# First attention heads in one set of streams with the recurrent half's output tiles

## The chip, the cores and the metric

One core of a Trainium2 chip runs the whole program. The time is device microseconds of one execution; the number given for the kernel before is the median of three. Engines are named as the profile names them: PE (TensorE: matmuls and transposes), DVE (VectorE), ACT (ScalarE), POOL (GpSimd), SP (SyncE, which issues the DMAs). PE writes its results to PSUM, which has eight banks here, each holding 128 x 512 float32.

## What is computed

One layer of a hybrid streaming encoder over 1024 prompt frames and 8 x 16 sample frames, together 1152 rows, or nine tiles of 128 rows (eight of the prompt, the ninth holds all samples). Cut to what matters:

```python
xr, gate, q, k, v, qi, ki, wi = split(rmsnorm(x) @ w_in)      # 1024 -> 2376 columns
y_a = rglru(conv(xr)) * gelu(gate)                            # recurrent half, 512 wide
q, k = rope(rmsnorm(q)), rope(rmsnorm(k))                     # 8 query heads, 2 key heads of 64
sel = topk(sum_h relu(qi_h . ki) * wi_h, 256)                 # sparse: the keys each frame may see
y_b = softmax(q . k[sel] / 8) @ v[sel]                        # attention half, 512 wide
x = x + concat(y_a, y_b) @ w_out                              # 1024 x 1024
x = x + (silu(h @ w1) * (h @ w2)) @ w_ffn_out                 # h = rmsnorm(x)
```

The attention is causal in chunks of 64 frames, so a query tile i of the prompt needs the key tiles 0 to i and no other. For query tiles 0 and 1 there are at most 256 keys, so no selection is needed and a fixed mask serves; tiles 2 to 8 need the mask that the top-k search makes.

## The kernel before, in words

The program is unrolled. Python generators, called streams, emit the instructions; `run(streams, width, side)` (line 93) keeps `width` streams active, always steps the oldest one that is due by its own estimate of time, and between the steps gives a turn to the side streams (weight loader, top-k search, key rotation, query normalisation and others). A stream that ends makes room for the next in the list. What comes out is an order of priority; a planner with a cost model of its own then fixes the order of instructions on each engine, allocates buffers and places the waits. On the chip each engine follows that order.

Stages, by time in the profile: normalisation and keys, index scores, then the recurrent half with the query projections beside it (to 408 us), then the output tiles of the recurrent half (408 to 474 us), the attention heads (474 to about 660 us), the output tiles of the attention half, and the feed-forward part (719 us to the end).

The pieces that the change touches:

- `out_tile_a(i)` (line 1341): the rows i of `y_a` times the upper half of `w_out`. Eight float32 matmuls 128x128 by 128x512 into two PSUM banks (each shows as two records in the trace), then two DVE additions into `acc[i]`. The four weight tiles `wa` hold four of the eight 4 KB slots of the pool `wr` until tile 8 is done. The last addition of tile 8 is kept as `wa_last`: the masks of tiles 6, 7 and 8 are emitted only once it exists, and on DVE are ordered behind it.
- `k_rope` (line 1249): a side stream that for each key tile i applies the rotation on POOL and DVE, writes the keys out, transposes them on PE and splits them into high and low parts, by two ACT copies and two DVE subtractions for each of the two key heads, into `k1` and `k2`. At the end `k_done` is set.
- `q_norm` (line 1236): multiplies the nine query tiles by their inverse norms on POOL.
- `attn(i, kv)` (line 1388): four query heads of query tile i on one key head. It waits until `k_done`, its mask and its queries are there. Then for each of the four: score matmuls, a DVE pass that adds the mask, scales and takes the maximum (`m`, `mx`), an exponential on ACT, a reciprocal on DVE, a multiplication on POOL. Then for each key tile: four PE transposes of `m`, a split by ACT and DVE, and three matmuls with the values; one ACT copy to `yF` ends it. The rows `m` take two of the `wr` slots where the width is at most 512, four above, and are taken in turn (`m_turn`).
- `sample_attn(b)`: the same for the 16 frames of stream b, against its cache.

The stage before the change runs as two calls: nine output tiles two at a time with `k_rope` and `q_norm` as side streams, a loop that drains these two, and then 24 heads and samples four at a time (`ATT_ORDER`: the heads of query tiles 0 to 5 first, those of 6 and 7 between the samples).

The key buffers `k1` and `k2` are allocated after the pool `tq` of the query projections is closed. Pools are stacked, so the keys stand where `tq`'s tiles stood (`tab`, `rp` and others of `q_tile`), and the first write to them waits for the last rotation of a query tile.

Of the kernel before, what the change touches and what calls it, by code (L numbers as in the profile page):

```python
# [10 lines left out]
F32R = mybir.dt.float32r  # L11
# [10 lines left out]
NT = 9  # L22
NP = 8
# [7 lines left out]
NB = 8  # L31
# [50 lines left out]
class Kernel:  # L82
# [183 lines left out]
    def build(self, upto=99):  # L266
        ctx, tc, nc, I, O = self.ctx, self.tc, self.nc, self.I, self.O
        L = "left"
        R = "right"
# [29 lines left out]
        def close():  # L299
            for st in (kist, tka, mid, yst, right):  # L300
                st.close()

        side = [self.loader()]
        with tc.tile_pool(name="t1a", bufs=2, side=R) as tp:
            g, wk = self.load_kv_weights(tp)
            side = self.run([self.norm_kv(i, tp, g, wk) for i in range(NT)], self.W_NORM, side)
# [7 lines left out]
        self.scored, self.masked, self.tk_done = set(), {0, 1}, set()  # L314
        self.qst, self.qst_t = {}, {}
        self.n_lru, self.spare, self.wa_last = 0, None, None
        self.m_turn, self.m_next, self.n_sa, self.in_att, self.k_done = 0, 0, 0, False, False
        self.n_idx, self.n_sidx, self.sidx, self.sq_done = 0, 0, None, False
        topks = [self.topk(g, p) for g, p in zip(groups, self.TK_PACE)]
        side += topks  # L320
# [1 line left out]
        with tc.tile_pool(name="t1b", bufs=2, side=R) as tp:  # L322
            self.qs = tp.tile([64, NB, 8, TS], F32, name="qs", bufs=1)
            st = {**{i: self.index(i, tp) for i in range(2, NT)}, **{("s", b): self.sample_index(b) for b in range(NB)}}
            side = self.run([st[x] for x in self.INDEX_ORDER], self.W_IDX, side + [self.sample_sel()])
# [6 lines left out]
        with tc.tile_pool(name="tq", bufs=2, side=R) as tp:  # L332
            queries = [[self.clock, g] for g in self.q_proj(tp)]
            with tc.tile_pool(name="lru", bufs=1, side=R) as lp:
                self.phase = 1
                side = self.run(self.lru(lp), 3, [self.lru_prep(lp)] + side, queries)
            self.phase = 2
            prep, lo = self.out_room(), self.lru_out()
            side = [x for x in self.run([g for _, g in queries], 3, [prep, lo] + side) if x is not prep]
# [4 lines left out]
        self.k1 = k_p.tile([128, 2, 1024], F32R, name="k1")  # L344
        self.k2 = k_p.tile([128, 2, 1024], F32R, name="k2")
        self.ksT = k_p.tile([128, 2, 128], F32R, name="ksT")
        with tc.tile_pool(name="woa", bufs=2, side=R) as tp:
            self.phase = 3
            kr, qr = self.k_rope(tp), self.q_norm(tp)
            side = self.run([self.out_tile_a(i) for i in range(NT)], 2, [prep] + side + [kr, qr])  # L350
            for x in (kr, qr):
                for _ in x:
                    pass
                side = [y for y in side if y is not x]
        if upto < 4:
            return close()
        with tc.tile_pool(name="att", bufs=1, side=R) as tp:
            self.in_att = True
            self.phase = 4
            self.smp = self.hblk.tile([128, 3 * D], F32, tag="h", name="smp")  # L360
            self.pT_free = [self.rest[:, 2048:3072]] + [self.smr[:, k * 1024:(k + 1) * 1024] for k in range(3)]
            self.pTn = tp.tile([128, 2, 128], F32R, name="pTn")
            self.kn1 = self.kn.rearrange("p i d -> p (i d)")
            self.mask01 = self.kn1[:, 896:1152]
            nc.gpsimd.memset(self.mask01, 0.0)
            nc.gpsimd.memset(self.mask01[0:64, 192:256], -BIG)
            st = {**{("s", b): self.sample_attn(b, tp) for b in range(NB)},
                  **{(i, kv): self.attn(i, kv, tp) for i in range(NP) for kv in range(2)}}
            self.smp_in = None
            side = self.run([st[x] for x in self.ATT_ORDER], self.W_ATT, side + [self.sample_prep()])  # L370
        mid.close()
        tka.close()
        if upto < 5:
# [3 lines left out]
        with tc.tile_pool(name="wob", bufs=2, side=R) as tp:  # L377
            self.gf = tp.tile([128, D], F32, name="gffn", bufs=1)
            nc.sync.dma_start(self.gf, I["norm_ffn"][None, :].to_broadcast([128, D]))
            self.half_b, self.hf_done, self.w1_first, self.first_ps = 0, set(), [], {}  # L380
            self.run([self.out_tile(i, tp) for i in range(NT)] + [self.ffn_start()], self.W_OUT,
                     [self.out_prep()] + side + [self.ffn_first()])
# [29 lines left out]
    LRU_LAT = 3.0  # L412
    K_LAT = 5.0
    W_ATT = 4
    W_OUT = 4
    INDEX_ORDER = (8, 2, 3, 4, ("s", 0), ("s", 1), 5, ("s", 2), ("s", 3), 6, ("s", 4), ("s", 5), 7, ("s", 6), ("s", 7))
    ATT_ORDER = (tuple((i, k) for i in range(6) for k in range(2)) + tuple(x for b in range(4) for x in ((6 + b // 2, b % 2), ("s", 2 * b), ("s", 2 * b + 1))))
# [831 lines left out]
    def k_rope(self, tp):  # L1249
        nc, I, O = self.nc, self.I, self.O  # L1250
        gk = self.load_g(tp, I["k_norm"], "gk")
        yield self.K_LAT
        v = self.kss.rearrange("p i a -> p (i a)")
        self.newton_rsqrt(v, v, tp, 2 * NT)
        rs = self.kss
        yield 0.5
        for i in range(NT):
            tab = self.tables(tp, i, gk, 1)
            self.begin()
            o = self.kn[:, i, :].rearrange("p (h d) -> p h d", h=2)  # L1260
            self.rope(o, o, tab, 2, tp, bufs=1)
            self.pool_tt(o, o, rs[:, i, :, None].to_broadcast([128, 2, 64]), ALU.mult)
            of = o.rearrange("p h d -> p (h d)")
            dst = O["k_p"][0, i * 128:(i + 1) * 128] if i < NP else O["k_s"].rearrange("b t k d -> (b t) k d")
            nc.sync.dma_start(dst.rearrange("t k d -> t (k d)"), of)
            t = self.end()
            yield 0.0
            yield from self.until(t)
            pt = self.ps()
            self.tr(pt[:, 0:128], of)  # L1270
            sl = slice(i * 128, (i + 1) * 128)
            if i == NP:
                self.split(self.ksT, pt[:, 0:128])
                self.k_done = True
                return
            for kv in range(2):

                a = slice(64 * kv, 64 * kv + 64)
                b = slice(64 - 64 * kv, 128 - 64 * kv)
                same, other = (self.k1, self.k2) if kv == 0 else (self.k2, self.k1)  # L1280
                h = same[a, kv, sl]
                nc.scalar.activation(h, pt[a, 0:128], AF.Copy)
                nc.scalar.activation(other[b, kv, sl], pt[a, 0:128], AF.Copy)
                nc.vector.tensor_tensor(other[a, kv, sl], pt[a, 0:128], h.bitcast(F32), op=ALU.subtract)
                nc.vector.tensor_tensor(same[b, kv, sl], pt[a, 0:128], h.bitcast(F32), op=ALU.subtract)
            yield 2.0


# [52 lines left out]
    def out_tile_a(self, i):  # L1341

        nc = self.nc
        nc.sync.dma_start(self.acc[i], self.x_src(i))
        w = []
        pos = [self.ps(), self.ps()]
        for c in range(4):
            w += yield from self.wait_w(("wa", c))
            for q in range(2):
                self.mm4(pos[q], self.yF[:, c, i * 128:(i + 1) * 128], w[c][:, q * 512:(q + 1) * 512], c == 0, c == 3)  # L1350
            yield 0.0
        if i == NT - 1:
            self.wused -= 4
        for q in range(2):
            a = self.acc[i][:, q * 512:(q + 1) * 512]
            x = nc.vector.tensor_tensor(a, pos[q], a, op=ALU.add)
            if q and i == NT - 1:
                self.wa_last = x.ins
            yield 0.4 if q else 0.0

    def out_tile(self, i, tp):
# [26 lines left out]
    def attn(self, i, kv, tp):  # L1388
# [2 lines left out]
        nch = 1 if W <= 512 else 2  # L1391
        n = W // nch
        mask = self.mask01[:, 256 - W:] if i < 2 else self.s[i]
        while not self.k_done or i not in self.masked or i not in self.q_ok or (kv and i not in self.qst):
            yield 0.5
        if kv == 0:
            self.begin()
# [355 lines left out]
```

## Time and profile before

| | |
|---|---|
| Median of three runs | 1537.71 us (1537.52 to 1539.65) |
| Profiled execution, its own time | 1536.94 us |
| Profiled execution, its span | 1535.1 us |
| PE busy | 1467.9 us (96%), 7786 matmuls |
| DVE busy | 865.2 us (56%) |
| ACT busy | 619.2 us (40%) |
| POOL busy | 269.7 us (18%) |
| Mean granted PE clock | 0.98 |

The chain that ended last goes through PE for 72% of the span and through DVE for 13%. A busy PE is not PE at its peak: the ends of matmuls are modelled, and a matmul at half clock counts as busy for twice the time, so the busy share has to be read beside the granted clock. The time of the profiled execution is 1.84 us more than its span.

### The profile page before, as it was taken

What the parts mean: (1) busy time and instruction counts of PE and PEld (TensorE: products, weight loads), DVE (VectorE), ACT (ScalarE), POOL (GpSimd) and SP (SyncE); (2) the same over time, 40 slices, a digit from 0 to 9 for tenths busy, and PEclk for the clock granted to TensorE, in tenths of its full rate; (3) what the DMA queues carried; (4) which work ended last, traced back from release to release, by engine and by line L of the source; (5) the groups of instructions that cost most, each with busy time, mean ns of one, the idle gap of its engine ahead of it and who ended that gap; (6) DMA issues with size and microseconds to landing.
All of it is one profiled execution on the core that took longest, in us unless ns stands there. A gap on an engine that the chain in (4) does not pass through costs nothing.

```text
span 1535.1 us, 20876 instructions
## 1 busy us (share of the span) xinstructions
PE 1467.9 (96%) x7786; PEld 1307.5 (85%) x7786; DVE 865.2 (56%) x1904; ACT 619.2 (40%) x1481; POOL 269.7 (18%) x425
## 2 busy tenths in 40 slices
PE   6889899889997999999999999999999999999998
PEld 6877688778745788889999998989898989898987
DVE  7556899899967988777233333342424242515233
ACT  5447988977415877745202020202121212111100
POOL 4214234333774544300000000000000000000000
PEclk8999899999998999999999999999999999999999
DMA  7201110010401002122102020202021111111003
GB/s 241 58 18 30 48 38 22 12 31 32 176 28 28 1 15 69 28 69 82 56 0 83 0 83 1 83 5 79 18 66 28 56 42 42 50 34 56 28 1 123
DMA packets 95093, 75.24 MB, mean 49 GB/s; under 512 B 13380, under 2 KB 85828, under 8 KB 94992
## 3 DMA queue, kind: packets, MB, share of 16 engines
q1 hardware_dynamic: 94992, 73.91, 15.9%
q8 instruction: 61, 1.00, 0.3%
q14 instruction: 40, 0.33, 0.1%
HBM read 67.62 MB, written 6.27 MB: 48 GB/s over the span
## 4 chain that ended last, share of the span: by engine, by line
PE 72%; DVE 13%; ACT 6%; issue 5%; POOL 2%; DMA 1%; SPq 0%; ACTq 0%; DVEq 0%; POOLq 0%
PE ps L207 66%; DVE junk L66 4%; PE ps L217 3%; ACT jk L66 3%; PE ps L212 3%; DVE tk_cand L66 2%; DVE tr L66 1%; ACT L66 1%; POOL rp L66 1%; DVE ti L66 1%; DVE qn L66 1%; ACT tr L66 1%; DVE m L66 1%; ACT relu L66 1%; DVE s L66 1%
## 5 line engine op out<-in xcount | busy, mean ns | idle before, releaser
L207 PE MATMUL ps<-hf,w 128*128 128x384 f32 x2556 | 453.1, 334 | 0.0
L207 PEld LDWEIGHTS ps<-hf,w 128*128 128x128 f32 x2556 | 444.2, 188 | 0.7
L207 PE MATMUL ps<-w,a 128*128 128x512 f32 x999 | 238.4, 389 | 0.0
L66 DVE TENSOR_TENSOR acc<-ps,acc 128x512 f32<-128x512 f32 x234 | 161.0, 690 | 118.2 <-PE ps L207 117.4
L207 PEld LDWEIGHTS ps<-w,a 128*128 128x128 f32 x999 | 187.3, 188 | 38.5
L66 ACT ACTIVATE w<-raw 128x512 fp32r<-128x512 f32 x124 | 75.2, 628 | 295.7 <-PE ps L207 219.2
L66 DVE TENSOR_TENSOR sg<-ps,sg 128x384 f32<-128x384 f32 x66 | 36.8, 557 | 276.7 <-PE ps L207 276.1
L66 ACT ACTIVATE a<-sg 128x384 fp32r<-128x384 f32 x66 | 34.5, 523 | 219.4 <-DVE sg L66 219.4
L66 DVE TENSOR_TENSOR w<-raw,w 128x512 fp32r<-128x512 f32 x116 | 76.9, 688 | 81.7 <-ACT w L66 81.5
L207 PE MATMUL ps<-hf,rest 128*128 128x384 f32 x612 | 114.3, 334 | 0.0
L66 ACT ACTIVATE jk<-s,tk_cand 128x384 bf16<-128x384 f32 (+3 forms) x128 | 99.5, 777 | 32.4 <-DVE tk_cand L66 29.7
L207 PEld LDWEIGHTS ps<-hf,rest 128*128 128x128 f32 x612 | 106.9, 188 | 0.2
L207 PE MATMUL ps<-h,w 128*128 128x384 f32 x576 | 106.7, 342 | 0.0
L207 PEld LDWEIGHTS ps<-h,w 128*128 128x128 f32 x576 | 100.4, 188 | 3.9 <-ACT relu L66 0.2
L207 PE MATMUL ps<-w,h 128*128 128x256 f32 (+1 forms) x600 | 97.7, 320 | 0.0
L207 PEld LDWEIGHTS ps<-w,h 128*128 128x128 f32 x600 | 85.1, 194 | 6.5
L66 ACT ACTIVATE sg<-ps 128x384 f32<-128x384 f32 x66 | 32.0, 486 | 119.7 <-PE ps L207 119.7
L212 PE MATMUL ps<-wa,yF 128*128 128x512 f32 x144 | 63.4, 593 | 2.4 <-DVE k L66 1.5
L66 POOL TENSOR_SCALAR m<-m,mx 128x128 f32<-128x128 f32 (+7 forms) x64 | 51.7, 814 | 54.1 <-DVE mx L66 45.2
L212 PEld LDWEIGHTS ps<-wa,yF 128*128 128x128 f32 x144 | 26.5, 190 | 35.5 <-issue 31.9
L66 ACT ACTIVATE m<-m,mx 128x128 f32<-128x128 f32 (+7 forms) x64 | 49.3, 771 | 16.4 <-DVE mx L66 16.0
L207 PE MATMUL ps<-k,qeo 128*128 128x384 f32 (+5 forms) x192 | 51.9, 383 | 3.7 <-DVE qeo L66 2.9
(266 smaller groups left out, 2139.8 us busy)
## 6 DMA issues: line engine op xcount, KB each, us to landing
raw<-in_w_ffn_in_dram SPq DMA_DIRECT2D x44, 512.0 KB
raw<-in_w_ffn_out_dram SPq DMA_DIRECT2D x22, 512.0 KB
raw<-in_w_in_dram SPq DMA_DIRECT2D x16, 512.0 KB
out_dram<-acc SPq DMA_DIRECT2D x9, 512.0 KB
x<-in_x_prompt_dram SPq DMA_DIRECT2D x8, 512.0 KB
acc<-in_x_prompt_dram SPq DMA_DIRECT2D x8, 512.0 KB
tab<-in_rope_dram SPq DMA_DIRECT2D x43, 64.0 KB
wa<-in_w_out_dram SPq DMA_DIRECT2D x4, 512.0 KB
```

The costliest lines, as they stand in the source:

```text
L66: return f(*args, **kw)
L207: self.nc.tensor.matmul(out, lhsT, rhs, start=start, stop=stop)
L212: self.nc.tensor.matmul(out, lhsT, rhs, start=start, stop=stop)
L217: self.nc.tensor.transpose(out, in_, self.ident[0:n, 0:n])
```

## The change

The two calls of `run` become one. The list begins with three output tiles (`OUT_FIRST`), then heads and output tiles alternate for six pairs, and the other heads and samples follow; four streams are active throughout. `k_rope` and `q_norm` stay side streams and are not drained. A head no longer waits for `k_done` but only until `k_tiles`, counted up as each key tile is split, is above its own query tile's number. The pool `att` is opened beside `woa`. The fixed mask `mask01` moves from the last columns of `kn` (key tiles 7 and 8, now still in use) to the end of `smp`. The phase number changes to 4 with the last output tile.

```diff
-        self.m_turn, self.m_next, self.n_sa, self.in_att, self.k_done = 0, 0, 0, False, False
+        self.m_turn, self.m_next, self.n_sa, self.k_done, self.k_tiles = 0, 0, 0, False, 0
...
-        with tc.tile_pool(name="woa", bufs=2, side=R) as tp:
+        with tc.tile_pool(name="woa", bufs=2, side=R) as tp, tc.tile_pool(name="att", bufs=1, side=R) as ap:
             self.phase = 3
-            kr, qr = self.k_rope(tp), self.q_norm(tp)
-            side = self.run([self.out_tile_a(i) for i in range(NT)], 2, [prep] + side + [kr, qr])
-            for x in (kr, qr):
-                for _ in x:
-                    pass
-                side = [y for y in side if y is not x]
-        if upto < 4:
-            return close()
-        with tc.tile_pool(name="att", bufs=1, side=R) as tp:
-            self.in_att = True
-            self.phase = 4
...
-            self.pTn = tp.tile([128, 2, 128], F32R, name="pTn")
+            self.pTn = ap.tile([128, 2, 128], F32R, name="pTn")
...
-            self.mask01 = self.kn1[:, 896:1152]
+            self.mask01 = self.smp[:, 2816:3072]
...
-            side = self.run([st[x] for x in self.ATT_ORDER], self.W_ATT, side + [self.sample_prep()])
+            outs, heads = [self.out_tile_a(i) for i in range(NT)], [st[x] for x in self.ATT_ORDER]
+            n = NT - self.OUT_FIRST
+            order = outs[:self.OUT_FIRST] + [x for p in zip(heads[:n], outs[self.OUT_FIRST:]) for x in p] + heads[n:]
+            side = self.run(order, self.W_ATT, [prep] + side + [self.k_rope(tp), self.q_norm(tp), self.sample_prep()])
...
+    OUT_FIRST = 3
...  # k_rope, behind the splits of a key tile
+            self.k_tiles += 1
...  # out_tile_a, with the last output tile
+                self.phase = 4
...  # attn
-        while not self.k_done or i not in self.masked or i not in self.q_ok or (kv and i not in self.qst):
+        while self.k_tiles <= i or i not in self.masked or i not in self.q_ok or (kv and i not in self.qst):
```

## Rows read from the trace of the kernel before

**Rows 1.** The page, part 2: busy tenths in 40 slices of 38.4 us; PEclk is the granted clock.

```profile
PE   6889899889997999999999999999999999999998
DVE  7556899899967988777233333342424242515233
PEclk8999899999998999999999999999999999999999
```

**Rows 2.** Busy time by stage, instructions in brackets; then granted PE clock, DMA share, GB/s.

```profile
408.00:443.00 35.00, 34.08 (x84) 15.00 (x83) 28.42 (x50) 2.59 (x14) 33.68 (x50) 1.00 0.09 25
443.00:474.00 31.00, 29.52 (x75) 13.06 (x74) 18.38 (x53) 7.73 (x30) 6.37 (x19) 1.00 0.16 45
474.00:520.00 46.00, 34.65 (x172) 28.07 (x171) 42.06 (x131) 35.76 (x94) 28.11 (x39) 0.81 0.02 6
520.00:640.00 120.00, 115.38 (x748) 100.70 (x747) 99.01 (x284) 92.69 (x216) 54.39 (x64) 1.00 0.12 36
```

**Rows 3.** The chain that ended last, in order of time: start, length, what.

```profile
719.30 811.35 PE ps L207 x4311
```

**Rows 4.** PE in order of time, 408 to 449 us; idle time and releaser in square brackets.

```profile
408.00 13.90 PE L212 MATMUL ps<-wa,yF 128*128 128x512 f32 x32
421.74 0.27 PE L217 MATMUL ps<-ident,kn 128*128 128x128 f32 x1
...
426.58 7.03 PE L212 MATMUL ps<-wa,yF 128*128 128x512 f32 x16
433.45 0.27 PE L217 MATMUL ps<-ident,kn 128*128 128x128 f32 x1
433.56 7.03 PE L212 MATMUL ps<-wa,yF 128*128 128x512 f32 x16
440.43 0.27 PE L217 MATMUL ps<-ident,kn 128*128 128x128 f32 x1
...
445.61 3.67 PE L212 MATMUL ps<-wa,yF 128*128 128x512 f32 x8 [1.48 <-DVE k L66]
```

**Rows 5.** PE in order of time, the first heads, 477 to 491 us.

```profile
477.69 4.57 PE L207 MATMUL ps<-k,qeo 128*128 128x128 f32 x18 [2.95 <-DVE qeo L66]
...
484.85 0.48 PE L217 MATMUL ps<-ident,m 128*128 128x128 f32 x1 [2.59 <-POOL m L66]
...
490.09 0.33 PE L217 MATMUL ps<-ident,m 128*128 128x128 f32 x1 [2.17 <-POOL m L66]
```

**Rows 6.** ACT in order of time, 421 to 447 us: the only row there.

```profile
441.92 4.02 ACT L66 ACTIVATE k<-ps 64x128 fp32r<-64x128 f32 x14 [32.13 <-DVE qn L66]
```

**Rows 7.** DVE in order of time, 437 to 447 us.

```profile
437.85 0.68 DVE L66 TENSOR_TENSOR acc<-ps,acc 128x512 f32<-128x512 f32 x1
...
441.33 0.43 DVE L66 TENSOR_TENSOR qn<-qn,rp 128x256 f32<-128x256 f32 x1
442.50 0.58 DVE L66 TENSOR_TENSOR k<-ps,k 64x128 fp32r<-64x128 f32 x2 [0.74 <-ACT k L66]
...
446.76 1.29 DVE L66 TENSOR_TENSOR acc<-ps,acc 128x512 f32<-128x512 f32 x2
```

**Rows 8.** The tiles of the mask work, 470 to 520 us: duration min/median/max in ns.

```profile
L66 DVE TENSOR_TENSOR_SCAN key<-junk x3: 1262/2015/2726, 474.9 to 502.0; 128x896 int16<-128x896 bf16 x1, 128x1024 int16<-128x1024 bf16 x1, 128x528 int16<-128x528 bf16 x1
L66 DVE SCALAR_TENSOR_TENSOR junk<-key,tk_cnt,junk x3: 810/1149/1493, 481.3 to 509.7; 128x896 bf16<-128x896 int16 x1, 128x1024 bf16<-128x1024 int16 x1, 128x528 bf16<-128x528 int16 x1
```

**Rows 9.** Busy time in stretches of 2 us around a stop of PE; columns as in rows 2.

```profile
488.00:490.00 2.00, 0.00 (x0) 0.00 (x0) 2.00 (x4) 0.58 (x3) 2.00 (x1) 1.00 0.00 0
490.00:492.00 2.00, 1.84 (x9) 1.35 (x10) 2.00 (x10) 1.45 (x4) 2.00 (x6) 0.75 0.00 0
492.00:494.00 2.00, 2.00 (x9) 1.71 (x8) 1.93 (x4) 1.98 (x6) 1.97 (x4) 0.50 0.00 0
494.00:496.00 2.00, 1.95 (x14) 1.65 (x13) 1.96 (x4) 1.19 (x3) 2.00 (x1) 0.90 0.47 131
```

More of the change, by code (lines that the diff above doesn't have):

```diff
@@ L346, in build @@
         self.ksT = k_p.tile([128, 2, 128], F32R, name="ksT")
-        with tc.tile_pool(name="woa", bufs=2, side=R) as tp:
+        with tc.tile_pool(name="woa", bufs=2, side=R) as tp, tc.tile_pool(name="att", bufs=1, side=R) as ap:
             self.phase = 3
-            kr, qr = self.k_rope(tp), self.q_norm(tp)
-            side = self.run([self.out_tile_a(i) for i in range(NT)], 2, [prep] + side + [kr, qr])
-            for x in (kr, qr):
-                for _ in x:
-                    pass
-                side = [y for y in side if y is not x]
-        if upto < 4:
-            return close()
-        with tc.tile_pool(name="att", bufs=1, side=R) as tp:
-            self.in_att = True
-            self.phase = 4
             self.smp = self.hblk.tile([128, 3 * D], F32, tag="h", name="smp")
             self.pT_free = [self.rest[:, 2048:3072]] + [self.smr[:, k * 1024:(k + 1) * 1024] for k in range(3)]
-            self.pTn = tp.tile([128, 2, 128], F32R, name="pTn")
+            self.pTn = ap.tile([128, 2, 128], F32R, name="pTn")
             self.kn1 = self.kn.rearrange("p i d -> p (i d)")
-            self.mask01 = self.kn1[:, 896:1152]
+            self.mask01 = self.smp[:, 2816:3072]
             nc.gpsimd.memset(self.mask01, 0.0)
             nc.gpsimd.memset(self.mask01[0:64, 192:256], -BIG)
-            st = {**{("s", b): self.sample_attn(b, tp) for b in range(NB)},
-                  **{(i, kv): self.attn(i, kv, tp) for i in range(NP) for kv in range(2)}}
+            st = {**{("s", b): self.sample_attn(b, ap) for b in range(NB)},
+                  **{(i, kv): self.attn(i, kv, ap) for i in range(NP) for kv in range(2)}}
             self.smp_in = None
-            side = self.run([st[x] for x in self.ATT_ORDER], self.W_ATT, side + [self.sample_prep()])
+            outs, heads = [self.out_tile_a(i) for i in range(NT)], [st[x] for x in self.ATT_ORDER]
+            n = NT - self.OUT_FIRST
+            order = outs[:self.OUT_FIRST] + [x for p in zip(heads[:n], outs[self.OUT_FIRST:]) for x in p] + heads[n:]
+            side = self.run(order, self.W_ATT, [prep] + side + [self.k_rope(tp), self.q_norm(tp), self.sample_prep()])
         mid.close()
```

## Prediction

> **What bounds the kernel now.** I read the slices of the page first, to see where PE is not the bound: from slice 19 on its digit stays at 9 and the granted clock at full, while the slices around 474 to 520 us are the last where the clock falls [rows 1]. The end of the chain of waits says the same: from 719 us to the end it is one unbroken run of matmuls [rows 3]. Nothing that moves earlier can shorten that run; it can only start sooner. So the change is worth what it takes out of the stretch between 408 us (first output tile) and 520 us, provided the stages behind stay bounded by the same work.
>
> The stages [rows 2] show four kinds of time. From 408 to 443 us PE is nearly full with output tiles, and so is POOL with rotations and masks: 33.7 of 35 us. From 443 to 474 us PE is full with output tiles and POOL, ACT and DVE have room (DVE 18.4 of 31 us). From 474 to 520 us it is the reverse: DVE is busy for 42.1 of 46 us, PE for 34.7 and this at a mean clock of 0.81. From 520 to 640 us PE is busy for 115.4 of 120 us at full clock, so 0.96 is what a well-filled attention stage reaches.
>
> What an output tile costs: 16 records, from one transposed key tile to the next 6.87 us (433.56 to 440.43), so 0.429 us a record [rows 4]. All nine are 144 records, 61.8 us of PE that no order removes.
>
> What the first heads cost on PE: 34.65 us busy times 0.81 is 28.1 us of work at full clock [rows 2]. So 46 - 28.1 = 17.9 us of the stretch is PE standing or half-clocked. The rows show it standing: 2.95 us before the first scores, 2.59 and 2.17 us before transposes that wait for POOL's multiplication [rows 5]. This is the room that output tiles could fill.
>
> **When the first head can start.** Not when its queries are normalised, but when its keys are split. The transposed first key tile leaves PE at 421.7 us [rows 4], yet ACT's first copy of it starts at 441.92 us, after 32 us idle, and is released by DVE's last query rotation [rows 6, 7]. That is the memory of the query projections' pool, on which the key buffers stand. The last rotation is late because POOL is full until then [rows 2]. The change touches none of this. The first DVE part of the key split ends at 443.1 us (442.50 + 0.58) [rows 7], and I take that as the earliest moment for scores after the change too.
>
> **Where PE will be then.** PE follows an order planned beforehand. In the order of before, DVE's first key splits stand between the additions of output tile 2 (437.85) and of output tile 3 (446.76) [rows 7], so the plan expects the keys while tile 3 is on PE, that is between records 48 and 64. On the chip those fall at 430.0 us (half way through the 16 records from 426.58) and 437.0 us [rows 4]. After three output tiles the heads are ahead of the rest in priority, so I expect their first scores at that place: PE then stands from 430.0 to 443.1 us (13.1 us) at worst, from 437.0 (6.1 us) at best of this reading, and from 433.5 (9.6 us) if the place is the middle, which I take, since nothing in the rows favours one end.
>
> **The sum.** At 443.1 us PE has still 144 - 56 = 88 records of output tiles, 37.8 us, and the 28.1 us of heads. At the 0.96 of the later stage, the nearest case of attention work with PE well fed, that is 65.9 / 0.96 = 68.6 us, so the state that before reached at 520 us is reached at 511.7: 8.3 us sooner. With the stop at record 48 (41.2 us of tiles left) it is 515.3 (4.7 sooner), at 64 (34.3 left) 508.1 (11.9 sooner).
>
> DVE gives the same from its side. Its work of 443 to 520 us is 18.4 + 42.1 = 60.5 us; at the 0.915 that it reached in the second part (42.1 / 46) it needs 66.1 us and ends at 509.2. PE is the later of the two, so PE's figure stands.
>
> What else moves. The masks of tiles 6 to 8 wait for the last output tile's addition, which now comes later. Three scans (1.26, 2.02, 2.73 us) and three selections (0.81, 1.15, 1.49 us), 9.5 us of DVE [rows 8], move behind it, towards 520 to 640 us, where DVE is busy for 99 of 120 us [rows 2] and PE sets the pace. First needed by the heads of tile 6, thirteenth in the list, they cost nothing there; with that cover gone they would cost up to their 9.5 us. The wait on key tiles instead of the last key: what stands behind the waiting scores on PE is the next output tile, and its DVE addition behind that; that is the stop priced above. Moving the fixed mask moves two POOL memsets, covered by POOL's wait for keys. The rotation's steps on POOL now share their queue with the heads' multiplications, and the tables they load come through SP in the same order as before: between 443 and 474 us POOL is busy for 6.4 of 31 us, so I price this at 0, with 0 and the 2.6 us of one wait of PE for POOL [rows 5] as ends. Four weight tiles keep four of the eight slots until the last output tile, so only two narrow heads are in flight instead of four; PE has output tiles to do meanwhile, so 0, and its price without that cover is in the third rival.
>
> The clock: after a stop of 2 us the next 6 us ran at 0.75, 0.50 and 0.90 [rows 9], a loss of 0.5 + 1.0 + 0.2 = 1.7 us. A stop of 9.6 us can cost that or some more. Against it, busy times clock overstates the heads' work, as a busy matmul counts up to its modelled end. The two have opposite signs and about one size; I leave both out and keep 2 us either way in the range.
>
> The profiled execution took 1536.94 us (its span and 1.84 us around it), 0.77 under the median of three. 1536.94 - 8.3 = **1528.6 us**.
>
> **Rivals.**
>
> *No stop.* The plan puts enough output tiles ahead of the first scores. Then PE has about 66 records left at 443.1, 28.3 us, and (28.3 + 28.1) / 0.96 = 58.8 us end at 501.9: 18.1 us sooner, 1518.8 us. For it: PE went through 443 us in before without standing, and the masks' 9.5 us leave DVE's sum in this stretch, so DVE (60.5 - 9.5, at 0.915: 55.7 us, 498.8) allows it. Against: the plan's expectation of the keys is early by 6 to 13 us.
>
> *No gain.* The stop takes what the filling gives: the heads sit on DVE and POOL as long as before, and the place for the scores is record 48 with PE at no more than 0.90 afterwards: 69.3 / 0.90 = 77.0, 520.1 us, so 1537 us. That the change doesn't do what it says belongs here: the plan may put the heads behind nearly all output tiles, since it too sees the key buffers come late, and then the order is that of before.
>
> *Slower.* PE runs its order with no overtaking, and each of the first six heads, two at a time in four slots, makes PE stand for its transposes. Rows of before have two such waits of 2.59 and 2.17 us [rows 5], 2.4 us on average, in a stage with four heads in flight. Six of them are 14.3 us, with 1.7 us of clock, behind a full stop of 13.1 us: 443.1 + 69.3 + 16.0 = 528.4, that is 8.4 us later than before, 1545.3 us. It decides from 7.6 us of standing after 443.1 (520 - 443.1 - 69.3). Against it: between these waits there are now output tiles that need no head.
> The Trainium skill ("TensorE: Matmul & The Clock Gate", section The mechanism) states that matmuls start and end in program order and only weight loads are pulled ahead. By that rule a score matmul that waits for its keys stops every output tile queued behind it. The trace agrees in so far as no matmul in rows 4 and 5 is seen to pass a waiting one, and it cannot show more, since before has no output tile queued behind a head.
>
> **How the numbers follow.** The forecast (a stop of 6 to 13 us, then well filled) 0.50, no stop 0.22, no gain 0.14, slower 0.14. A change of 0.2%, 3.1 us, is about the least that a measurement of this kernel tells from none. The first two are faster: 0.72. No gain is within it: 0.14. Slower: 0.14. The forecast's own range is 1525.0 less 2 to 1532.2 plus 2, so 1523 to 1534. The range for all reaches down to the no-stop case less 2 us, 1516.8, and up past no gain, into the slower case: 1517 to 1541.
>
> **What would show it.** Right: on PE a stop that ends at about 443 us and is released by key splits (`k`) or by `qeo`; behind it output-tile records mixed with scores; the clock between 474 and 520 us near 1.00; `yF` of the first head well before 493; the last output tile's record at 485 to 500 us instead of 473; the unbroken run of matmuls starting near 711 us and as long as before (811 us). The forecast is wrong if PE never stands before 443 us, if the run starts at 716 us or later, or if that run's length changes: the cause would then lie outside this stretch.

## The result, and the profile after

The changed kernel takes 1546.37 us (median of 4 runs, 1546.19 to 1548.07) against 1537.62 us before in the same comparison: ratio 1.0060, 95% interval 1.0047 to 1.0072. It is slower by some 9 us; the forecast was 8.3 us faster.

The chain of waits of the changed kernel still ends in one run of matmuls (start, length, what):

```profile
730.27 811.35 PE ps L207 x4311
```

It is as long as before and starts 11.0 us later [rows 3]. So the whole loss lies ahead of 730 us, in the stretch that the change rearranges and the one behind it. (The two profiled executions, 1548.07 and 1536.94 us, lie 11.1 us apart, the medians 8.75; the traces show some 2 us more than the usual loss.) The slices of the page:

```profile
PE   6889899889979899999999999999999999999998
DVE  7556899899875988678324233333424242424243
PEclk9999899999989899999999999999999999999999
```

Slices are 38.65 us. On PE the twelfth (425 to 464 us) fell from 9 to 7 and the thirteenth rose from 7 to 9; the clock, which in this stretch had its dip in the thirteenth alone, now dips in the twelfth and the fourteenth [rows 1]. The stages, columns as in [rows 2]:

```profile
408.00:443.00 35.00, 28.16 (x70) 11.90 (x68) 29.74 (x51) 1.97 (x8) 33.58 (x49) 1.00 0.08 24
443.00:474.00 31.00, 24.75 (x81) 13.96 (x82) 23.24 (x83) 16.33 (x54) 12.44 (x32) 0.83 0.21 71
474.00:520.00 46.00, 41.39 (x159) 25.58 (x159) 32.34 (x85) 23.57 (x59) 13.42 (x18) 0.93 0.00 1
520.00:640.00 120.00, 112.39 (x713) 97.89 (x712) 101.37 (x292) 91.74 (x211) 58.80 (x68) 0.99 0.12 34
640.00:719.00 79.00, 75.73 (x412) 64.06 (x411) 57.38 (x122) 43.08 (x92) 4.34 (x5) 0.98 0.17 47
```

The third stage did fill: PE 41.4 of 46 us at 0.93, before 34.7 at 0.81. The first two lost more than it won, and the last two, where nothing was expected, lost as well. The last of them in the kernel before, for comparison:

```profile
640.00:719.00 79.00, 78.81 (x427) 67.64 (x426) 59.46 (x125) 42.40 (x87) 0.80 (x1) 1.00 0.19 54
```

PE in order of time, after the change:

```profile
407.03 13.90 PE L212 MATMUL ps<-wa,yF 128*128 128x512 f32 x32
...
424.91 2.84 PE L212 MATMUL ps<-wa,yF 128*128 128x512 f32 x6 [2.54 <-DVE acc L66]
...
433.54 5.32 PE L212 MATMUL ps<-wa,yF 128*128 128x512 f32 x12
446.52 1.08 PE L207 MATMUL ps<-k,qeo 128*128 128x128 f32 x4 [7.67 <-ACT k L66]
...
448.97 7.93 PE L212 MATMUL ps<-wa,yF 128*128 128x512 f32 x12
...
471.72 0.50 PE L207 MATMUL ps<-smr,vhl 128*128 128x512 f32 x1 [2.23 <-ACT smr L66]
...
498.23 3.59 PE L212 MATMUL ps<-wa,yF 128*128 128x512 f32 x8
```

After 64 records of output tiles the first scores stand at the head of PE's queue and wait 7.67 us for their keys, with 80 records behind them that need nothing. (The Trainium skill, "TensorE: Matmul & The Clock Gate", section The mechanism, says that matmuls start and end in program order; this row agrees, with a wait of 7.67 us; the kernel before had no output tile queued behind a waiting head.) What they wait for is ACT's copies of key tiles, the first of which as before comes right behind DVE's last query rotation:

```profile
444.53 1.71 ACT L66 ACTIVATE k<-ps 64x128 fp32r<-64x128 f32 x6 [11.57 <-DVE qn L66]
```

That rotation itself ends later, at 444.45 us in place of 441.76 [rows 7]: between its two halves DVE now splits the first head's queries (`qeo`), which the changed order brings there.

```profile
442.60 1.39 DVE L66 TENSOR_TENSOR qeo<-ps,qeo 64x512 fp32r<-64x512 f32 x2
444.02 0.43 DVE L66 TENSOR_TENSOR qn<-qn,rp 128x256 f32<-128x256 f32 x1
```

The 12 records after the stop take 7.93 us where 12 took 5.32 before it. The stretches of 2 us show why: PE is busy throughout from 450 us and the granted clock (the column behind the engines) is 0.50 until 454, that is 1.2 GHz in place of 2.4:

```profile
442.00:444.00 2.00, 0.00 (x0) 0.00 (x0) 1.95 (x3) 0.00 (x0) 1.02 (x3) 0.95 0.00 0
444.00:446.00 2.00, 0.00 (x0) 0.00 (x0) 1.91 (x4) 1.37 (x6) 1.09 (x2) 0.50 0.12 37
...
450.00:452.00 2.00, 2.00 (x4) 0.97 (x3) 2.00 (x11) 0.61 (x4) 0.40 (x1) 0.50 0.11 33
452.00:454.00 2.00, 2.00 (x3) 0.70 (x3) 1.35 (x7) 1.32 (x7) 1.70 (x5) 0.50 0.11 33
454.00:456.00 2.00, 2.00 (x6) 0.88 (x5) 1.31 (x3) 0.00 (x0) 1.38 (x4) 0.99 0.12 33
```

Where a time has several such causes I add up the 2 us stretches of this view: what PE stood in each, and what half clock cost it there (its busy time, times one less the granted clock). Their sum is called *lost* below. From the first output tile, which starts between 405.0 and 411.8 us, to the last run every kernel in the table has about the same work on PE, 284 to 287 us, so that start and the lost time together explain the end. Each line is one execution; eighteen executions of the kernel before, side by side, spread over 5.3 us, so differences of 2 or 3 us between lines show nothing by themselves. Lost, in us, and the start of the last run:

```
kernel                                   408-443  443-520  520-719  last run
before                                     0.9     19.6      4.8     719.3
changed                                    6.8     16.6     14.0     730.3
 + key tiles apart                         7.6     12.5     15.4     727.6
 + all nine tiles first                    3.1     19.8      7.9     725.5
 + six tiles first                         4.4     16.7      5.4     719.1
 + masks not ordered                       8.8     19.5      9.9     734.0
 + masks from tile 5 on                    8.7     19.4     13.3     730.6
before, masks behind head 8                2.7      8.9     20.8     723.9
before, masks from tile 5 on               1.9     17.8      9.6     722.0
before, masks from tile 4 on               2.1     16.5      8.9     718.9
```

The change pays 5.9 us in the first stage, wins 3.0 in the second and loses 9.2 in the third; a start of the first tile 1.0 us earlier (407.03 against 408.00) gives some of that back. That leaves 11.1 us, about the 11.0 at the end.

What PE stood for, summed over 405 to 720 us, names two kinds of wait. One is the stop for the keys. The other is ACT's copies of probabilities (`smr`, and `rest`, which is used alike). Their group of matmuls after the change, then before; the last figures are the idle time ahead of them and what ended it:

```profile
L207 PE MATMUL ps<-smr,vhl 128*128 128x512 f32 x162 | 56.4, 434 | 7.4 <-ACT smr L66 7.4
L207 PE MATMUL ps<-smr,vhl 128*128 128x512 f32 x162 | 53.7, 416 | 1.8 <-ACT smr L66 1.3 <-DVE smr L66 0.4
```

With `rest` these copies cost 9.2 us of standing in place of 1.9, the first scores' wait for keys 8.2 in place of none; waits for POOL's multiplications fell from 6.5 to 3.1.

### The profile page after: what moved, and what is told of

The parts are those of the page before. It is cut to its first block, busy times and chain, and to the rows that moved or that the text cites. A ratio compares the mean times of both kernels' runs of the same rounds, so it can differ in the third digit from the quotient of the medians.

```text
span 1546.0 us, 20863 instructions
## 1 busy us (share of the span) xinstructions
PE 1468.0 (95%) x7786; PEld 1304.8 (84%) x7786; DVE 868.1 (56%) x1904; ACT 620.2 (40%) x1481; POOL 267.2 (17%) x425
## 4 chain that ended last, share of the span: by engine, by line
PE 72%; DVE 12%; ACT 7%; issue 5%; POOL 2%; DMA 1%; SPq 0%; DVEq 0%; ACTq 0%; POOLq 0%
PE ps L207 66%; DVE junk L66 4%; PE ps L212 3%; PE ps L217 3%; ACT jk L66 3%; DVE tk_cand L66 2%; DVE tr L66 1%; ACT L66 1%; ACT relu L66 1%; DVE ti L66 1%; ACT tr L66 1%; POOL qn L66 1%; POOL rp L66 1%; ACT yF L66 0%; DMA x<-in_x_prompt_dram 0%
## 5 line engine op out<-in xcount | busy, mean ns | idle before, releaser
L212 PE MATMUL ps<-wa,yF 128*128 128x512 f32 x144 | 66.9, 614 | 2.5 <-DVE acc L66 2.5
L207 PE MATMUL ps<-smr,vhl 128*128 128x512 f32 x162 | 56.4, 434 | 7.4 <-ACT smr L66 7.4
```

The source lines that it names most:

```text
L207: self.nc.tensor.matmul(out, lhsT, rhs, start=start, stop=stop)
L212: self.nc.tensor.matmul(out, lhsT, rhs, start=start, stop=stop)
```

## The experiments

Each ran in 5 rounds beside the kernel before. The theories in the expectations: A, the stop for the keys, which stand on the memory of the query projections; B, the masks of row tiles 6 to 8, which follow the last output tile and now fall among heads; D, that only two heads are in flight while the output tiles hold their slots. The rivals S (the masks are harmless where they are, the loss is the stop) and C (DVE has no room anywhere in this stretch) come up in the last two groups.

**The keys in memory of their own.** In the changed kernel, and in the kernel before as a control, the key tiles are pushed off the projections' memory:

```
+        pool(mid, "gap", R).tile([128, 768], F32, name="gap")
         k_p = pool(mid, "kst", R)
```

> The changed kernel, with a gap of 3 KB under the key buffers so that they no longer stand where the query rotations' tiles stood; nothing else. Theory A (the stop: PE stood 7.7 us before the first scores until the keys were split, and its clock was half until about 454 us, together 11 to 13 us): the stop goes, the clock stays full, 1533 to 1537 us. Theory B (the mixing itself: after the last output tile the heads refill as slowly as before, with the masks of tiles 6 to 8 among them, so no room is filled): the stop goes but what is won is lost behind the last output tile, 1542 to 1546 us. Theory C (other parts of the edit, such as the pools and the moved mask): no change, 1546 us.

> The kernel before, with the same gap of 3 KB under the key buffers. In it PE waits for keys only once, 1.5 us. All theories: 1535 to 1538 us; anything below would say that the gap is worth something by itself.

Changed: 1545.37 us, 1.0057 (1.0043 to 1.0071). Before: 1536.92, 1.0001 (0.9992 to 1.0010). The stop in the changed kernel is less than half, and what ends it is now the first head's queries:

```profile
442.08 1.48 PE L207 MATMUL ps<-k,qeo 128*128 128x128 f32 x4 [3.36 <-DVE qeo L66]
```

Yet the time hardly moves. The two stages to 520 us lose 20.1 us in place of 23.4, the last loses 1.4 more. The half clock still comes, behind the shorter stop (0.50 from 442 to 448 us). Theory A, which gave 1533 to 1537 us, falls as the whole cause: with less than half of the wait the order is about as slow. The run did not remove the stop, so what the rest of it costs is not shown here.

**How many output tiles stand first.**

```
-    OUT_FIRST = 3
+    OUT_FIRST = 9          (second kernel: 6)
```

> The changed kernel with OUT_FIRST = 9: all nine output tiles ahead of the heads, so one call and all other edits, but no mixing. Theories A and B: as before, 1535 to 1540 us. Theory C: 1544 us or more.

> The changed kernel with OUT_FIRST = 6: the first scores come behind six output tiles, later than the keys, and only three tiles (20.6 us) are mixed with the first heads. Theory A (the stop before the keys and the half clock behind it are the loss): no stop, the three tiles fill the 18 us that PE lost behind the last tile in the kernel before, 1526 to 1533 us. Theory B (the masks of tiles 6 to 8, ordered behind the last tile's addition, make PE stand among the wider heads, wherever that addition is): no stop, but 8 to 12 us lost behind the last tile, 1535 to 1541 us.

Nine first, which is the order of before with the rest of the edit: 1540.72 us, 1.0024 (1.0014 to 1.0034), just above the 1535 to 1540 of theories A and B. So about 3.5 us of the loss comes without any mixing, with the other parts (one set of streams, pools open together, a plan that comes out otherwise), and some 5.5 with the order. How much of either is only the plan's coming out otherwise is not told apart: that alone moves the time by some 3 us, as the next group shows. Six first: 1537.99, 1.0003 (0.9994 to 1.0012), level with before and 0.2% faster than nine first, inside theory B's range and outside A's. With six, the first scores wait 1.79 us, and the last stage loses 5.4 us, near the 4.8 of before, not 14.0. Mixing is thus not bad in itself; with three tiles first it loses, with six it does not.

**The masks, earlier and later.** First not ordered at all behind the output tiles:

```
-            while self.wa_last is None:
-                yield 0.5
+            pass
...
-                if not g["act"]:
-                    st.enter_context(self.tc.issue_after(self.wa_last))
```

Then a condition that was meant to hold them back until the eighth head (in the changed kernel, there with the keys apart, and in the kernel before):

```
-            while self.wa_last is None:
+            while self.wa_last is None or self.m_turn < 8:
```

> The changed kernel, with the masks of tiles 6 to 8 no longer held until the last output tile's addition (neither emitted after it nor ordered behind it on DVE). Theory B: the refill after the last output tile becomes quick, 6 to 9 us less, 1537 to 1540 us. Theory A: the stop stays, 1544 to 1548 us, and it may grow, since the masks then run on DVE and POOL while these are full with rotations.

> The changed kernel, with the masks of tiles 6 to 8 held until eight heads have taken their turn (instead of only until the last output tile). Theory A: the stop stays and with it the loss, 1545 to 1548 us. Theory B: of the 15 us that PE lost to standing and half clock from the last tile to the twelfth head, 6 to 10 go, 1536 to 1541 us, unless the masks cost the same among the heads of tiles 4 and 5.

> Both edits: the gap under the key buffers and the masks held until eight heads have taken their turn. Theory A alone: as with the gap alone, 1544 to 1547 us. Theory B alone: as with the late masks alone. Both together, each with its part: 1532 to 1537 us. If it stays above 1541 us, a third cause (two heads in flight while the weights hold four slots) must hold the rest.

> The kernel before, with the masks of tiles 6 to 8 held until eight heads have taken their turn. Theory B: part of its 18 us behind the last tile is the masks', and among later heads they cost less or the same: 1530 to 1538 us. Theory A says nothing of it: 1536 to 1539 us.

Not ordered: 1552.77 us, 1.0103 (1.0089 to 1.0117). The scans now run from 405 to 435 us, where POOL and DVE make keys and queries, and PE waits once each 8.0 us for a key split, 5.5 for POOL's rotation and 5.1 for a DVE step on `jk`, a work tile of the top-k search; the first output tile, too, starts 4.8 us later than in the changed kernel (411.80). The other three (1549.78, 1.0080; with keys apart 1545.73, 1.0056; in the kernel before 1539.45, 1.0014) did not do what they were for: the plan put the masks where they had been (scans from 500.2, 498.2 and 473.7 us). They show that a plan which comes out a little otherwise moves the time by some 3 us (ratio 1.0080 against 1.0060).

Next the masks were tied to the eighth head's last reciprocal, in three kernels:

```
-            while self.wa_last is None:
+            while self.mask_at is None:
...
-                    st.enter_context(self.tc.issue_after(self.wa_last))
+                    st.enter_context(self.tc.issue_after(self.mask_at))
...
-            nc.vector.reciprocal(mx[:, 3:4], mx[:, 3:4])
+            r = nc.vector.reciprocal(mx[:, 3:4], mx[:, 3:4])
+            if turn == 7 and j == 3:
+                self.mask_at = r.ins
```

> The changed kernel, with the masks of tiles 6 to 8 ordered on DVE behind the last reciprocal of the eighth head instead of behind the last output tile's addition; in the planned order of DVE they now stand two query tiles later (the run that held them back by turns alone had left them where they were). Theory B (the masks make PE stand behind the last output tile): 5 to 9 us come back, 1537 to 1541 us. Theory B' (they cost the same among any wide heads, and were free only in the kernel before, where nothing else was ready): 1545 to 1549 us.

> The kernel before, with the same order: the masks behind the eighth head. Theory B: the 18 us that PE lost at the start of the heads shrink by 5 to 9 and the masks cost little later, 1529 to 1534 us. Theory B': the start gets shorter and the later heads longer by as much, 1536 to 1540 us.

> Six output tiles first and the masks behind the eighth head. Theory B: neither a stop for keys nor the masks among the first heads, 1527 to 1533 us. Theory B': as with six tiles first alone, 1536 to 1540 us.

All are slower than the same kernel without the tie: changed 1553.57 us, 1.0097 (1.0083 to 1.0112); before 1542.44, 1.0036 (1.0022 to 1.0049); six first 1546.87, 1.0064 (1.0051 to 1.0077). The kernel before shows the price best. Its windows, with the masks' scans now at 510.9 to 538.6 us:

```profile
443.00:520.00 77.00, 71.07 (x315) 48.85 (x316) 59.43 (x194) 49.12 (x131) 29.20 (x57) 0.96 0.06 18
520.00:719.00 199.00, 183.44 (x1067) 157.19 (x1068) 156.23 (x385) 125.77 (x282) 57.09 (x65) 0.97 0.15 42
```

Without masks PE is busy 71.1 us of the second stage at 0.96; the kernel before has 64.2 at 0.89 there. The sixth head ends at 506.6 us in place of 522.0. Behind 520 us, among the wider heads, 16 us more are lost (20.8 against 4.8), against 10.7 won. Some 12 of the 16 fall between 520 and 558 us, beside and right behind the masks: DVE's second scan takes 2.72 us from 524.25, and a cast of the samples' preparation, which starts once the masks are emitted, 2.32 us from 532.66; PE then stands 2.41 us for DVE's `smr`, which comes behind that cast. Near 640 us come 2.8 more; the wait there, 3.05 us for POOL's `smp`, is in the kernel before too, but here half clock follows it, and nothing ties that to the masks.

**Two heads in flight.** The changed kernel, four narrow score rows in one slot in place of two:

```
-        per = 2 if nch == 1 else 1
+        per = 4 if W <= 256 else 2 if nch == 1 else 1
...
-            m = ms[:, 512 * (j % per):]
+            m = ms[:, 1024 // per * (j % per):]
```

> The changed kernel, with the four rows of a head of tiles 0 and 1 in one slot instead of two, so that with four slots held by the weights four such heads can be in flight instead of two. Theory D (two heads in flight is what slows the first heads): 1537 to 1542 us. Theories A and B: 1544 to 1548 us.

1547.45 us, 1.0066 (1.0054 to 1.0078); the stop (7.68 us) and PE's waits for copies of probabilities are as in the changed kernel. PE's order came out nearly the same too, with the first scores behind the same 64 records, and the edit leaves the heads from query tile 2 on at two slots. So slots for the first four heads are not what holds them up. Whether more heads in flight would help was not tested: this part of theory D stays open.

**The masks ahead of the heads.** They may start at the addition of an earlier output tile (index 4, the fifth; index 3, the fourth):

```
-            if q and i == NT - 1:
+            if q and i == 4:
                 self.wa_last = x.ins
```

(in the changed kernel `self.phase = 4` stays with the last tile).

> The kernel before, with one constant changed: the masks of row tiles 6 to 8 may be built from the fifth output tile's addition on, not the ninth's, so that they run among output tiles 5 to 8 (about 450 to 474 us), where DVE and POOL have room. Theory B (the part lost behind the last output tile is the masks running in order among the heads): the first six heads end near 507 to 513 us in place of 522, and nothing later is held up: 1523 to 1531 us. Rival S (the masks are harmless where they are, and the whole loss of the change is the stop for the keys): 1535 to 1540 us. Second rival (the masks hold up the output tiles' additions, and with them PE): 1540 to 1546 us.

> The changed kernel (three output tiles first) with the masks allowed from the fifth output tile's addition on; the first heads then run beside them. Theory B: the stop before the first scores stays (7 to 10 us with the half clock behind it), the stretch from the last output tile to the twelfth head gets the some 8 us back: 1534 to 1541 us. Rival S: 1544 to 1549 us. Third reading (what DVE's masks cost is the same wherever heads run, and heads now run there too): 1546 to 1553 us, as where the masks were not ordered at all.

> The changed kernel with six output tiles before the first head (the version that took 1538.0 us) and the masks allowed from the fifth output tile's addition on. Theory B: the masks leave the heads, 1524 to 1533 us. Rival S: 1535 to 1541 us, as with six tiles first alone.

> As the second, with the key tiles in memory of their own. With the masks gone from the heads, theory B expects what is left of the mixing to show: 1522 to 1532 us. If the keys' place still matters with six tiles first it is faster than the second by 2 to 4 us; if not, the two agree within 2 us. Rival S: 1533 to 1541 us.

Before: 1537.95 us, 0.9998 (0.9990 to 1.0007). Changed: 1548.86, 1.0073 (1.0060 to 1.0085). Six first: 1544.17, 1.0038 (1.0024 to 1.0052); with keys apart too 1540.53, 1.0023 (1.0013 to 1.0033). None did what theory B expected. Rival S gave the right range for three of the four (not for six first, 1544.17), but not by its reason, as the kernel before shows. Its six first heads went from first scores to the sixth result in 33.5 us (486.70 to 520.20) where they had taken 44.3 (477.69 to 521.95): with the masks out of the way they were 10.8 faster. But the first scores came 9.0 us later. DVE in order of time:

```profile
476.56 0.77 DVE L66 SCALAR_TENSOR_TENSOR junk<-key,tk_cnt,junk 128x528 bf16<-128x528 int16 x1
479.40 0.62 DVE L66 CAST junk<-s 128x528 bf16<-128x528 f32 x1 [2.08 <-POOL s L66]
...
480.54 0.69 DVE L66 TENSOR_TENSOR acc<-ps,acc 128x512 f32<-128x512 f32 x1
```

and PE behind it:

```profile
481.29 1.97 PE L217 MATMUL ps<-ident,qn 128*128 128x128 f32 x8 [5.30 <-DVE acc L66]
486.70 4.57 PE L207 MATMUL ps<-k,qeo 128*128 128x128 f32 x18 [3.44 <-DVE qeo L66]
```

Behind the last scan and selection a copy of the ninth tile's finished mask waits on DVE 2.08 us for POOL; four additions and the key splits stand behind it in DVE's queue, and PE stands 5.30 us for an addition and 3.44 more for the queries. The price was not saved, it was paid at another place. (The expectations further down call this copy the masks' last step. By the source it belongs to `sample_prep`: the samples need it, from the fourteenth place of the list on. Putting it behind the first heads was not tried.) In the changed kernel it is the same: lost 19.4 us in place of 16.6 from 443 to 520 us, and only 0.7 less behind. With six first the first scores wait 7.36 us for queries, and 7.32 with the keys apart too; so the 3.6 us between these two (1544.17 and 1540.53) are not the keys' wait, though they fit what was expected of it.

Last, one tile sooner still, and a changed order with seven tiles first.

> The kernel before with the masks of row tiles 6 to 8 allowed from the fourth output tile's addition on, one tile sooner than in the run that took 1537.9 us. There the six first heads took 33.5 us from their first scores in place of 44.3, but the masks' last step stood on DVE ahead of the last four additions (a wait of 2.1 us for POOL among them), PE stopped 5.3 us for an addition, and the first scores came 9 us later. Theory B (DVE runs in order, and the masks cost PE only where what stands behind them is needed at once): with the masks over two tiles before the end, the additions catch up, the first scores come at 478 to 481 us, the sixth head ends at 511 to 515: 1526 to 1532 us. Rival C (DVE has no room anywhere between 408 and 522 us, so 9.5 us of masks cost about that wherever they stand): 1535 to 1541 us.

> The changed kernel with seven output tiles before the first head, the masks allowed from the fourth output tile's addition on (so all of them stand ahead of the first head's additions on DVE), and the key tiles in memory of their own. Theory B: mixing is left with what it can fill, the last two tiles under the first heads, and neither the keys nor the masks stop it: 1523 to 1532 us. Rival C: 1534 to 1541 us, as with six tiles first.

Before with the masks from the fourth tile on: **1534.67 us, 0.9975 (0.9964 to 0.9985)**, 3.7 us faster than the kernel before and the fastest of all here. The wait for POOL still comes (2.07 us at 473.7) and PE still stands for the queries, but earlier:

```profile
475.50 0.30 PE L217 MATMUL ps<-ident,kn 128*128 128x128 f32 x1 [1.86 <-DVE acc L66]
475.63 1.88 PE L212 MATMUL ps<-wa,yF 128*128 128x512 f32 x4
483.36 4.57 PE L207 MATMUL ps<-k,qeo 128*128 128x128 f32 x18 [4.05 <-DVE qeo L66]
```

It falls short of theory B's 1526 to 1532, since the first scores come at 483.4, not 478 to 481; the sixth head ends at 516.9. Its profiled execution, at 1536.62 us, is the slowest of its 8 runs and only 0.3 under that of before, so the trace accounts for little of the gain that the times show. Seven first: 1540.40, 1.0011 (1.0002 to 1.0021), within rival C's range; 1534.67 is 0.3 us below C's and 2.7 above B's. C is nearer than B: moving 9.5 us of masks into the best place found brought 3.7.

## Why the prediction was wrong

**Right.** The last run starts when the stretch ahead lets it and keeps its length (811.35 us). PE meets the first scores at record 64, the late end of the place that I gave, stands there, and is released by a key split; 7.67 us is inside 6.1 to 13.1. The time 1546.4 lies near the slower rival's 1545.3, but not by its mechanism: PE's waits for POOL's multiplications are 3.1 us in all from 405 to 720 us (6.5 before), not 14.3. Of the signs that I named, the first head's result came at 469.5 us, well before 493, and the last output tile's record ended at 501.8, just past the 485 to 500; the clock from 474 to 520 was 0.93, not near 1.00, and a last run from 716 us or later was to show the forecast wrong: it is 730.

**First failing step: "At the 0.96 of the later stage".** Up to the end of the stop the sum came out, by luck: two errors cancel. The stop ended at 446.52, 3.4 us after my 443.1, and "the change touches none of this" was wrong: 1.4 of the 3.4 us are the query split on DVE above. But 64 records were done by then, not 56, and the 8 are 3.4 us of tiles. So 80 records are left, 34.3 us at 0.429 [rows 4], and the 28.1 us of heads [rows 2]: 62.4 us. At 0.96 they would be done at 511.5, the working's 511.7. The state in question came at some 523 us: the sixth head's result is at 525.1 where before had it at 522.0. So they took some 77 us, a rate of 0.81, and the step is worth 11.5 us. Of the 13 us lost after the stop up to 520 (16.6 of the table less the 3.5 of the stop behind 443), 5.8 are half clock. I had left the clock out, with 2 us either way, from a stop of 2 us [rows 9]; behind the 7.67 us stop it stood at 0.50 until 454 us, and it fell again between 512 and 520. The other 7.3 are standing, 4.4 of it for ACT's copies of probabilities (2.23 us in the row at 471.72). The rate of 0.96 came from a stage of wider heads without output tiles; narrow heads beside output tiles don't reach it. The sum on DVE's side, 0.915, failed likewise: DVE is busy 55.6 of 77 us, 0.72. Neither engine's total set the pace; the rows show short waits from engine to engine instead.

**Second failing step: the masks "cost nothing there".** I called 520 to 640 us covered because PE sets the pace there. The kernel before with its masks tied behind head 8 is that very move, and lost some 12 us more beside them, of 16 in all behind 520 us, against 10.7 won ahead of it: the cover didn't hold, and the term that I put at 0 came to more than the 9.5 us that I gave as its price without cover. In the changed kernel the scans start from 503.5 to 525.8 us, and short stops of PE stand beside them and the samples' preparation that comes with them. POOL:

```profile
519.55 2.15 POOL L66 TENSOR_TENSOR s<-junk 128x1024 f32<-128x1024 bf16 x1 [1.58 <-DVE junk L66]
521.79 1.37 POOL L66 TENSOR_SCALAR s<-s 128x1024 f32<-128x1024 f32 x1
524.32 0.69 POOL L66 TENSOR_SCALAR m<-m,mx 128x512 f32<-128x512 f32 x1 [1.16 <-DVE mx L66]
```

and PE, which needs that `m` for its transposes:

```profile
525.07 0.44 PE L217 MATMUL ps<-ident,m 128*128 128x128 f32 x2 [0.98 <-POOL m L66]
526.07 0.44 PE L217 MATMUL ps<-ident,m 128*128 128x128 f32 x2 [0.56 <-POOL m L66]
527.96 0.50 PE L207 MATMUL ps<-rest,vhl 128*128 128x512 f32 x1 [1.45 <-ACT rest L66]
```

The maxima `mx` that POOL waits for stand on DVE behind the cast of the samples' preparation (1.66 us from 520.59), and the third scan (1.29 us from 525.82) stands between the last maximum of one head and the first of the next. Three short stops, 3.0 us, and half clock behind them (1.7 us lost).

**But the masks alone don't explain the 9.2 us lost behind 520.** The changed kernel with its masks ahead of 485 us still loses 13.3 us there. Between 508 and 538 us, where the changed kernel has its masks and loses 10.7 us, that one still loses 9.2, and the kernel before 1.1: the masks' presence makes little of it. What goes with the loss in most runs is the number of tiles ahead of the first head: with three first 13.3 to 16.9 us (as changed, keys apart, masks from tile 5, four rows in a slot, and the two that held the masks back by turns; 18.9 with the masks tied to head 8, but 9.9 with them not ordered), with six or more 5.4 to 11.5 as long as the masks aren't late. PE's waits there are mostly single ones of 1 to 2.4 us for ACT's copies of probabilities, and dips of the clock behind them. That the heads, started one by one between output tiles, run on with less overlap would fit, but which choice of the plan makes these waits wasn't isolated. The cause of these waits stays open, and with it most of the 9 us behind 520.

**"No stop" and the rival of no gain.** Six tiles first is close to the case that I called no stop (its stop is 1.79 us) and was given 1518.8 us; it took 1538.0. So the stop alone was not what kept the gain away. What fits the runs, though no one run isolates it, is that masks, additions and heads share DVE's and POOL's queues wherever they are put.

## What to carry to other kernels

Before filling one stage's idle PE with another stage's matmuls, list what else is tied to the end of the moved work (here the masks) and price it at its new place as it stands in the queues there, not by which engine has the longer sum (here it was put at 0, and moving the masks alone cost some 12 us). A mean rate of a neighbouring stage is no forecast for a mixture: take it from a stretch with the same short chains, and add the half clock behind each stop. Try the cheap reorderings first: one constant for the masks' place gained 3.7 us, where the mixing of heads and tiles lost 9 us with three tiles first and none with six.

## What the hardware showed beside this

The granted clock came back later after the longer stop: three stretches of 2 us below full after a stop of some 2 us [rows 9], five at 0.50 from 444 us on around the end of the 7.67 us stop, in the last two of which PE was already busy throughout. But the length of one stop does not decide it: behind four stops of 0.3 to 1.2 us between 509 and 516 us the clock stood at 0.52, 0.50, 0.50 and 0.77 from 512 to 520.

One and the same cast on DVE, 128x1024, of the samples' preparation, took 0.69 us in the kernel before with the masks from tile 5 on and 1.66 us in the changed kernel, each time without a recorded wait.

```profile
470.89 0.69 DVE L66 CAST key<-ident 128x1024 bf16<-128x1024 f32 x1
```

```profile
520.59 1.66 DVE L66 CAST key<-ident 128x1024 bf16<-128x1024 f32 x1
```

The traces show what goes with it. In 15 of the 20 kernels POOL's addition `s<-junk` (2.11 to 2.16 us; the row at 519.55 above) was running when the cast began. In every one the cast ended 0.54 to 0.65 us after that addition, and so took anything from 0.68 to 2.33 us. In three the cast began first: it took 0.68 or 0.69 us, and POOL's addition then took 2.56 to 2.64. So these two instructions held each other up, and the profile records no wait for it. A price taken from durations on DVE alone therefore depends on what POOL runs beside it.
